# Score and meta products over all 128 array rows, and head pairs side by side, in a four-layer kernel

## The chip, the cores and the metric

The kernel runs on one core of a Trainium2 chip. TensorE multiplies (a weight load puts the stationary operand into its 128 x 128 array, a matmul streams the moving operand through it), VectorE (DVE) and ScalarE (ACT) work on what it leaves in PSUM, GpSimd (POOL) does small jobs in SBUF, SyncE (SP) issues DMAs. The metric is the device time of one execution in microseconds (us), the median of several runs.

## What is computed

Two small transformers run one after the other on 256 tokens of width 1024, in float32. The first has layer A (latent attention with a gated convolution), an MLP, layer C (sparse attention over compressed, selected and windowed keys) and an MLP. The second sees the 256 tokens behind 16 meta tokens and has layer AB (attention over selected keys, beside gated linear attention) and layer CD (retention beside stick-breaking attention). With 256 tokens all four blocks of layer C are always selected and its window reaches every earlier token. Cut to what the change touches:

```python
# layer C, group g, head r of a group
sc = q @ kc.T * scale - slope * (t - centre)     # compressed keys, 15 of them
o_cmp = softmax(sc) @ vc
o_slc = softmax(q @ ks.T * scale - slope * dist) @ vs
o_win = softmax(q @ kw.T * scale - slope * d) @ vw
out = g0 * o_cmp + g1 * o_slc + g2 * o_win
# layer AB: choice of the keys, attention, gated linear attention
score = einsum('qhs,qh->qs', relu(iq @ ik.T), iw)        # 8 heads of 64, top 64 keys are kept
oa = softmax(aq @ ak.T * scale + bias) @ av              # 8 heads of 64, meta keys among them
ob = tril(q_t @ k_t.T) @ v + q_t @ S_before              # 4 heads, chunks of 64
# layer CD
oc = (q @ k.T * decay) @ v                               # 4 heads of 64, values of 128
od = stick_breaking(dq @ dk.T) @ dv                      # 8 heads of 64
```

## The kernel before, in words

Everything is held transposed: features on the 128 partitions, tokens along a row. Weight matrices stream from HBM in halves of 512 KB; ACT and DVE split each into a high and a low part (lines 289 and 290), and the projections (`proj`, `take2`, `tiles2`, `acc_block`) multiply three of the four products of parts (`mm3`). Operands of type float32r go through TensorE once, plain float32 operands show as two matmuls each. Nearly every matmul is issued by the helper `mm` (line 328), so rows are told apart by their tiles. The program is handed to a scheduler that sets the order of each engine's instructions; each engine then works its list in that order. PSUM has eight banks: two called `d`, two called `m`, four called `w`.

A matmul uses as many rows of the array as its operands have partitions, and as many columns as its stationary operand is wide. The profile gives this as rows*columns: 128*128 for a projection, 64*128 for a product over one head of 64, 32*128 or 16*128 for products over meta or compressed keys, 128*64 where one head's values are the stationary operand.

What the change touches, by line:

- **Layer C** (`layer_c`, line 905 on). For a pair p of heads, `nsa_scores` takes for each head and each half t of the queries a product with the high part of the keys (`kh`, 128 rows: the queries' high part sits on 64 of them, their low part on the other 64) and one with the low part (`kl`, the 64 rows of the head alone) into the same PSUM tile, 256 keys wide for t = 0 and 512 for t = 1. `nsa_compress` makes the compressed keys and values once, the values masked by head into `vbd` (four DVE instructions, line 1068). `nsa_out` starts a pair's output with one product of `vbd` and the compressed weights `pct` over 32 rows, then multiplies with values per head (128*64).
- **Layer AB** (`layer_ab`). `select` takes the 8 products of `iq` and `ik` one by one for each half of the queries, each over 64 rows. `dsa_scores` takes a pair's scores per head and half, each into a PSUM bank of its own; pairs 0 to 2 use `w` banks, pair 3 the two `d` banks. `dsa_out` starts with a product of `vb` and `pmt` over 32 rows. `gla` works through a pair of heads one after the other: scores (`kg`, `qg`, 64 rows), a mask on DVE, products with values, products with the states `st` (64*64).
- **Layer CD** (`layer_cd`). `stick_pair` already puts the two heads of a pair side by side. `stick_out` starts with a product of `vb` and `wm` over 32 rows; `retention` starts a head's output with two products of `am` and the meta values over 16 rows.

Of the kernel before, what the change touches and what calls it, by code (L numbers as in the profile page):

```python
# [86 lines left out]
def _const_c():  # L87
# [18 lines left out]
    half = ((np.arange(128)[:, None] // 16) % 2 == np.arange(2)[None, :]).astype(np.float64)  # L106
# [46 lines left out]
def _const_cd():  # L153
# [17 lines left out]
    half = np.zeros((128, 2))  # L171
    for i in range(64):
        rep[15 - i % 16, i] = 1.0
        half[i, (i // 16) % 2] = 1.0
# [135 lines left out]
class K:  # L310
# [593 lines left out]
    def layer_c(self, xh, xl):  # L904
        nc, tc = self.nc, self.tc
        with tc.tile_pool(name="lc", bufs=1) as lp, tc.tile_pool(name="lc2", bufs=2) as l2:
# [5 lines left out]
            cw, cs = tile([128, 96], "cw"), tile([128, 516], "cs")  # L912
# [7 lines left out]
            kbd, vbd = tile([128, 2, 32], "kbd"), tile([128, 2, 2, 64], "vbd")  # L920
# [5 lines left out]
            for gp in range(2):  # L926
# [40 lines left out]
            self.nsa_gates(xh, xl, r, cs[:, 512:514], gt, lp)  # L967
            self.nsa_compress(self.psum("d"), blk, w1, cw, cs[:, 514:516], kbd, vbd, lp)
# [26 lines left out]
    def nsa_gates(self, xh, xl, r, has, gt, lp):  # L995
# [3 lines left out]
        ge = lp.tile([48, SEQ], F32, name="ge")  # L999
# [33 lines left out]
    def nsa_compress(self, ps, blk, w1, cw, half, kbd, vbd, lp):  # L1033
# [25 lines left out]
        for gg, s in enumerate(HALVES):  # L1059
            nc.vector.tensor_copy(kbd[s, :, 16 * gg:16 * gg + 16], kp[s].rearrange("p (gp n) -> p gp n", gp=2))  # L1060
        hr = lp.tile([128, 2, 4, 32], F32, name="hr")
        nc.vector.tensor_copy(
            hr[64:128], hg[64:128].rearrange("p gp gg n -> p gp (gg n)")[:, :, None, :].broadcast_to([64, 2, 4, 32]))
        for gp in range(2):
# [30 lines left out]
    def nsa_scores(self, p, q2, kh, kl, gt, l2, bank):  # L1095
# [6 lines left out]
        for gg in range(2):  # L1102
            st = l2.tile([128, 2, 2, 2], F32, tag=f"st{gg}", name=f"st{gg}")
            h = HALVES[gg]
            pm = []
            for t in range(2):
# [3 lines left out]
                self.mm(s, q[h], kl[h, gp, :256 * (t + 1)], False, True)  # L1110
# [31 lines left out]
    def nsa_out(self, p, pts, vt, vbd, pct, mh, ml):  # L1142
        gp, r = p // 4, p % 4
        o = self.psum("m")[:, :SEQ]
        q = slice(32 * r, 32 * r + 32)
        self.mm(o, vbd[q, gp].rearrange("p g d -> p (g d)"), pct[q, gp].rearrange("p t n -> p (t n)"), True, False)
# [24 lines left out]
    def values(self, xh, xl, r, pool, l2, name):  # L1171

        v = pool.tile([128, 3, 512], F32, tag="tok", name=name)
        tmp = []
# [173 lines left out]
    def select(self, nz, ps, r, mk, iq, gp, l2):  # L1348
# [32 lines left out]
    def gla(self, j, qg, kg, kdt, bvt, dec, cau, mix, gp):  # L1381
# [20 lines left out]
        for hf in range(2):  # L1402
            h = 2 * j + hf
            hs = slice(64 * hf, 64 * hf + 64)
            p = self.psum("w")
            for t in range(2):
                ts = slice(16 + 128 * t, 144 + 128 * t)
                self.mm(p[:, 128 * t:128 * t + 128], kg[hs, j, ts], qg[hs, j, ts])
            self.mm(p[0:16, 256:272], kg[hs, j, 0:16], qg[hs, j, 0:16])
# [5 lines left out]
            o = self.psum("w")[:, :384]  # L1415
            vs = slice(128 * h, 128 * h + 128)
# [3 lines left out]
            for c in range(4):  # L1420
                self.mm(o[64 * (c % 2):64 * (c % 2) + 64, 128 * (c // 2):128 * (c // 2) + 128],
                        qg[hs, j, 16 + 64 * c:80 + 64 * c], st[hs, c], False, c >= 2)
            ob = gp.tile([128, 384], F32, tag="gob", name="gob")
# [21 lines left out]
    def dsa_meta(self, aq, ak, avt, skew, rep, half, dp):  # L1445
# [4 lines left out]
        vb = dp.tile([32, 4, 2, 64], F32, tag="vb", name="vb", bufs=1)  # L1450
        pv = p.rearrange("p (a b c) -> p a b c", a=4, b=2)
        for g in range(2):
            nc.vector.tensor_scalar(vb[:, :, g], pv[:, :, g], half[0:32, g:g + 1], None, op0=OP.mult)
# [24 lines left out]
    def dsa_scores(self, pr, aq, ak, skew, mk, dp, bank):  # L1478
# [3 lines left out]
        pmeta = dp.tile([128, 2, 2, 16], F32, tag="pmeta", name="pmeta")  # L1482
        for g in range(2):
            h = 2 * pr + g
            hs = slice(64 * g, 64 * g + 64)
# [30 lines left out]
        pmt = dp.tile([32, 256], F32, tag="pmt", name="pmt")  # L1516
        nc.scalar.activation(pmt, p[0:32, :256], AF.Copy)
# [25 lines left out]
    def layer_cd(self, xh, xl, x):  # L1543
# [3 lines left out]
        with tc.tile_pool(name="cd", bufs=1) as lp, tc.tile_pool(name="cd2", bufs=2) as l2, \  # L1547
                tc.tile_pool(name="cd4", bufs=4) as l4:
            tile = lambda shape, name: lp.tile(shape, F32, name=name)
            ccd = tile([128, 2 * T2 + 3 * 128 + 66], "ccd")  # L1550
# [6 lines left out]
            cuts = np.cumsum([0, T2, T2, 128, 128, 128, 64, 2]).tolist()  # L1557
# [87 lines left out]
            vb = tile([64, 4, 2, 64], "vb")  # L1645
            for g in range(2):
                nc.vector.tensor_scalar(vb[:, :, g], p.rearrange("p (a b c) -> p a b c", a=4, b=2)[:, :, g],
                                        half[0:64, g:g + 1], None, op0=OP.mult)
# [3 lines left out]
            self.stick_out(0, wts, vb, dvr, mix, l2)  # L1652
            stick(2)
            rotary(cq, r, S)
            cvt = self.values(xh, xl, r, l2, l2, "cvt")
            ret = lambda j: self.retention(j, ck, cq, cvt, dect, l2)
# [235 lines left out]
```

## Time and profile before

| what | us |
|---|---|
| median of 3 runs (1009.80 to 1014.47) | 1012.83 |
| the profiled execution, device time | 1015.24 |
| its span, first to last instruction | 1013.5 |
| PE busy, of the span | 986.9 |
| DVE busy | 669.7 |
| ACT busy | 517.6 |
| POOL busy | 86.2 |

The profile is one execution. Busy time of PE is modelled from sizes, and matmuls overlap in a pipeline, so the duration of a row says little; what a matmul costs is read from the start of one row to the start of the next. A row of the timeline merges neighbours of one kind (x2), and the time to the next row's start is then that of all of them. PEclk is the clock granted to TensorE as a share of its full 2.4 GHz; 0.50 is its other level, 1.2 GHz.

### The profile page before, as it was taken

What the parts mean: (1) busy time and instruction counts of PE and PEld (TensorE: products, weight loads), DVE (VectorE), ACT (ScalarE), POOL (GpSimd) and SP (SyncE); (2) the same over time, 40 slices, a digit from 0 to 9 for tenths busy, and PEclk for the clock granted to TensorE, in tenths of its full rate; (3) what the DMA queues carried; (4) which work ended last, traced back from release to release, by engine and by line L of the source; (5) the groups of instructions that cost most, each with busy time, mean ns of one, the idle gap of its engine ahead of it and who ended that gap; (6) DMA issues with size and microseconds to landing.
All of it is one profiled execution on the core that took longest, in us unless ns stands there. A gap on an engine that the chain in (4) does not pass through costs nothing.

```text
span 1013.5 us, 19176 instructions
## 1 busy us (share of the span) xinstructions
PE 986.9 (97%) x7638; PEld 913.8 (90%) x7638; DVE 669.7 (66%) x1372; ACT 517.6 (51%) x933; POOL 86.2 (9%) x112
## 2 busy tenths in 40 slices
PE   7999999999999989999999999999999999999996
PEld 6999989999998967877999999988898679998985
DVE  6889486555555898674855555568977655757752
ACT  6646365444444667564644444455535335454442
POOL 1120010000001000001000000010211201003121
PEclk9999999999999999899899999999999789999999
DMA  9744347555553544211465555547354213643301
GB/s 331 246 163 146 133 139 266 169 193 200 185 172 116 189 156 139 95 58 42 132 235 197 181 175 181 191 143 240 111 172 137 94 43 98 235 129 122 105 1 42
DMA packets 46074, 154.64 MB, mean 153 GB/s; under 512 B 6424, under 2 KB 7968, under 8 KB 45856
## 3 DMA queue, kind: packets, MB, share of 16 engines
q1 hardware_dynamic: 45552, 152.85, 45.1%
q8 instruction: 60, 0.98, 0.4%
q10 hardware_dynamic: 432, 0.57, 0.2%
q14 instruction: 30, 0.25, 0.1%
HBM read 152.33 MB, written 2.70 MB: 153 GB/s over the span
## 4 chain that ended last, share of the span: by engine, by line
PE 94%; DVE 2%; DMA 1%; ACT 1%; issue 1%; POOL 1%; SPq 0%; POOLq 0%; ACTq 0%; DVEq 0%
PE pd L328 46%; PE pw L328 39%; PE pm L328 6%; PE pm L1133 1%; PE pm L1165 1%; DMA x<-in_xT 1%; DMA st<-in_ab_in 1%; POOL rc L389 0%; DVE st L290 0%; PE pm L1506 0%; DVE x L521 0%; PE pm L1704 0%; DVE zz L1027 0%; ACT st L289 0%; PE pw L881 0%
## 5 line engine op out<-in xcount | busy, mean ns | idle before, releaser
L290 DVE TENSOR_TENSOR st<-st,st 128x1024 fp32r<-128x1024 f32 (+2 forms) x274 | 326.6, 1210 | 168.9 <-ACT st L289 168.4
L289 ACT ACTIVATE st<-st 128x1024 fp32r<-128x1024 f32 (+2 forms) x274 | 279.5, 1041 | 276.4 <-PE pd L328 138.8
L328 PE MATMUL pd<-xh,st 128*128 128x256 f32 (+1 forms) x1856 | 360.0, 288 | 8.6 <-ACT st L289 6.3
L328 PEld LDWEIGHTS pd<-xh,st 128*128 128x128 f32 x1856 | 295.4, 191 | 16.7 <-ACT st L289 6.3
L328 PE MATMUL pd<-xl,st 128*128 128x256 f32 (+1 forms) x928 | 265.6, 288 | 0.0
L328 PE MATMUL pw<-hh,st 128*128 128x256 f32 x1024 | 188.4, 283 | 0.0
L328 PEld LDWEIGHTS pd<-xl,st 128*128 128x128 f32 x928 | 177.3, 191 | 2.5 <-issue 1.0
L328 PEld LDWEIGHTS pw<-hh,st 128*128 128x128 f32 x1024 | 161.1, 191 | 0.0
L328 PE MATMUL pw<-hl,st 128*128 128x256 f32 x512 | 144.6, 283 | 0.0
L328 PEld LDWEIGHTS pw<-hl,st 128*128 128x128 f32 x512 | 98.0, 191 | 0.0
L328 PE MATMUL pd<-akq,st 128*128 128x272 f32 (+1 forms) x384 | 78.0, 293 | 0.0
L328 PE MATMUL pw<-xh,st 128*128 128x256 f32 (+1 forms) x384 | 75.1, 285 | 0.8 <-ACT xh L533 0.8
L328 PEld LDWEIGHTS pd<-akq,st 128*128 128x128 f32 x384 | 61.0, 188 | 2.5 <-issue 1.9
L328 PEld LDWEIGHTS pw<-xh,st 128*128 128x128 f32 x384 | 61.2, 189 | 1.4 <-ACT xh L533 1.2
L328 PE MATMUL pd<-gs,st 128*128 128x272 f32 (+1 forms) x192 | 55.3, 288 | 0.0
L328 PE MATMUL pw<-xl,st 128*128 128x256 f32 (+1 forms) x192 | 53.9, 283 | 0.0
L328 PE MATMUL pw<-mh,st 128*128 128x256 f32 x256 | 51.1, 294 | 0.1
L389 POOL TENSOR_TENSOR rc<-rc,mhalf 128x2 f32<-128x2 f32 (+4 forms) x17 | 21.2, 1254 | 323.1 <-DVE rc L386 319.1
L328 PEld LDWEIGHTS pw<-mh,st 128*128 128x128 f32 x256 | 41.8, 197 | 1.3 <-issue 0.6
L487 POOL TENSOR_TENSOR sq<-sq 128x256 f32<-128x256 f32 x12 | 8.9, 740 | 336.1 <-ACT sq L485 335.2
L328 PE MATMUL pw<-ml,st 128*128 128x256 f32 x128 | 37.2, 297 | 0.0
L328 PEld LDWEIGHTS pd<-gs,st 128*128 128x128 f32 x192 | 36.2, 189 | 0.5 <-issue 0.4
(450 smaller groups left out, 1366.8 us busy)
## 6 DMA issues: line engine op xcount, KB each, us to landing
st<-in_w SPq DMA_DIRECT2D x128, 512.0 KB, 4.5
st<-in_ab_in SPq DMA_DIRECT2D x32, 512.0 KB, 3.9
st<-in_cd_in SPq DMA_DIRECT2D x28, 512.0 KB, 4.5
st<-in_a_in SPq DMA_DIRECT2D x18, 512.0 KB, 6.9
st<-in_c_in SPq DMA_DIRECT2D x16, 512.0 KB, 4.6
st<-in_a_out SPq DMA_DIRECT2D x8, 512.0 KB, 5.2
st<-in_c_out SPq DMA_DIRECT2D x8, 512.0 KB, 3.8
st<-in_ab_out SPq DMA_DIRECT2D x8, 512.0 KB, 3.8
```

The source lines that it names most:

```text
L289: self.last = self.nc.scalar.activation(hi[:, p], raw[:, p], AF.Copy).ins
L290: self.nc.vector.tensor_tensor(lo[:, p], raw[:, p], hi[:, p].bitcast(F32), op=OP.subtract)
L328: self.pe = self.nc.tensor.matmul(out, lhsT, rhs, start=start, stop=stop, skip_group_check=True).ins
L389: nc.gpsimd.tensor_tensor(r, r, self.mhalf[:p, :n], op=OP.pow)
L487: add = lambda e, a, b: e.tensor_tensor(self.sqs[a], self.sqs[a], self.sqs[b], op=OP.add)
L1133: nc.tensor.transpose(tp[:, 128 * j:128 * j + 128], src, self.ident)
L1165: nc.tensor.transpose(ps[:b - a, 128 * j:128 * j + 128], x[:, a:b], self.ident)
```

## The change

1. Products over few rows become products over all 128 rows, with zeros in the rows that do not belong: `kl` gets a copy per head that is zero on the other head's 64 rows; `vbd` becomes a tile of eight masked copies of the values for each two key groups, of which a pair of heads multiplies two with all of `pct`; `vb`, `pmt`, `wmt`, `am` and the meta part of `cvt` are 128 rows high and cleared on POOL. Two DVE instructions on 128x512 replace the four of line 1068.
2. Products over 64 rows are issued in pairs, one head on the upper and one on the lower half of the array, into two PSUM banks: in `select`, in `dsa_scores` (where both halves of the queries now share one bank per head), and in `gla` (scores of both heads, then masks, then values, then states alternating between the heads).
3. Three scratch tiles move into rotating buffers that exist already (`ge`, `hr`, `vbd`).

```diff
             kh = lp.tile([128, 2, 2, 512], F32R, name="kh")
-            kl = lp.tile([128, 2, 512], F32R, name="kl")
+            kl = lp.tile([128, 2, 2, 512], F32R, name="kl")
+            for gg, h in enumerate(HALVES):
+                nc.gpsimd.memset(kl.bitcast(F32)[HALVES[1 - gg], :, gg], 0.0)
...
-                    nc.vector.tensor_tensor(kl[h, gp], k[h], kh[h, gp, gg].bitcast(F32), op=OP.subtract)
+                    nc.vector.tensor_tensor(kl[h, gp, gg], k[h], kh[h, gp, gg].bitcast(F32), op=OP.subtract)
...
-            for gg in range(2):
-                nc.vector.tensor_scalar(vbd[:, gp, gg], vp, half[:, gg:gg + 1], None, op0=OP.mult)
+
+            v = self.pair(SEQ, "sq", bufs=4).rearrange("p a (b d) -> p (a b) d", d=64)
+            nc.vector.tensor_tensor(v, vp[:, None, :].broadcast_to([128, 8, 64]),
+                                    half[:, :, None].broadcast_to([128, 8, 64]), op=OP.mult)
+            vbd.append(v)
...
-                self.mm(s, q[h], kl[h, gp, :256 * (t + 1)], False, True)
+                self.mm(s, q, kl[:, gp, gg, :256 * (t + 1)], False, True)
...
-        self.mm(o, vbd[q, gp].rearrange("p g d -> p (g d)"), pct[q, gp].rearrange("p t n -> p (t n)"), True, False)
+        self.mm(o, vbd[gp][:, 2 * r:2 * r + 2].rearrange("p g d -> p (g d)"), pct[:, gp].rearrange("p t n -> p (t n)"),
+                True, False)
...
-                hs = slice(64 * (h % 2), 64 * (h % 2) + 64)
-                p = self.psum("w")[:, :wd]
-                self.mm(p, iq[hs, h // 2, 16 + 128 * t:144 + 128 * t], ik[hs, :wd])
+
+                if h % 2 == 0:
+                    two = [self.psum("w")[:, :wd] for _ in range(2)]
+                    for p, hs in zip(two, HALVES):
+                        self.mm(p, iq[hs, h // 2, 16 + 128 * t:144 + 128 * t], ik[hs, :wd])
+                p = two[h % 2]
...
+        ps, os2, ats = [[self.psum("w") for _ in range(2)] for _ in range(2)] + [[]]
+        for t in range(2):
+            ts = slice(16 + 128 * t, 144 + 128 * t)
+            for p, hs in zip(ps, HALVES):
+                self.mm(p[:, 128 * t:128 * t + 128], kg[hs, j, ts], qg[hs, j, ts], t == 0, False)
...
-            for c in range(4):
+        for c in range(4):
+            for o, hs in zip(os2, HALVES):
                 self.mm(o[64 * (c % 2):64 * (c % 2) + 64, 128 * (c // 2):128 * (c // 2) + 128],
                         qg[hs, j, 16 + 64 * c:80 + 64 * c], st[hs, c], False, c >= 2)
...
-        vb = dp.tile([32, 4, 2, 64], F32, tag="vb", name="vb", bufs=1)
+        vb = dp.tile([128, 4, 2, 64], F32, tag="vb", name="vb", bufs=1)
+        self.pmts = [dp.tile([128, 256], F32, name=f"pmt{i}", bufs=1) for i in range(2)]
+        for v in (vb, *self.pmts):
+            nc.gpsimd.memset(v, 0.0)
...
+        parts = (0, 0, 144), (1, 144, 416)
+        ss = [self.psum(bank)[:, :416] for _ in range(2)]
+        for t, c, d in parts:
+            for s, hs in zip(ss, HALVES):
+                self.mm(s[:, c:d], aq[hs, pr, 16 + 128 * t:144 + 128 * t], ak[hs, pr, :d - c], t == 0, t == 1)
...
-            for t, wd in ((0, 144), (1, 272)):
-                s = self.psum(bank)[:, :wd]
-                self.mm(s, aq[hs, pr, 16 + 128 * t:144 + 128 * t], ak[hs, pr, :wd])
+            for t, c, d in parts:
+                s, wd = ss[g][:, c:d], d - c
...
+            vb = tile([128, 4, 2, 64], "vb")
+            wmt, am = tile([128, 256], "wmt"), tile([128, 2, 256], "am")
+            for v in (vb, wmt, am):
+                nc.gpsimd.memset(v, 0.0)
...
-            self.mm(o, vb[32 * pr:32 * pr + 32, P].rearrange("p a b -> p (a b)"), wm[32 * pr:32 * pr + 32], True, False)
+            self.mm(o, vb[:, P].rearrange("p a b -> p (a b)"), wm, True, False)
...
-                self.mm(o[:, c:c + 128], am[:, f, 128 * t:128 * t + 128], cvt[0:16, 0, vs], c == 0, False)
+                self.mm(o[:, c:c + 128], am[:, f, 128 * t:128 * t + 128], cvt[:, 0, vs], c == 0, False)
```

## Rows read from the trace of the kernel before

**Rows 1.** The page: span, busy time of PE, the chain that ended last by engine, and the costliest group of weight loads (busy us, mean ns of one, idle before it).

```profile
span 1013.5 us, 19176 instructions
PE 986.9 (97%) x7638; PEld 913.8 (90%) x7638; DVE 669.7 (66%) x1372; ACT 517.6 (51%) x933; POOL 86.2 (9%) x112
...
PE 94%; DVE 2%; DMA 1%; ACT 1%; issue 1%; POOL 1%; SPq 0%; POOLq 0%; ACTq 0%; DVEq 0%
...
L328 PEld LDWEIGHTS pd<-xh,st 128*128 128x128 f32 x1856 | 295.4, 191 | 16.7 <-ACT st L289 6.3
```

**Rows 2.** Busy time of each engine by stretch (us from the span's start, length, then PE, PEld, DVE, ACT, POOL busy, the granted clock, DMA share, GB/s): the two parts of layer C's attention, and two of the stretches with the lower clock, in layer C and in layer AB.

```profile
366.00:424.00 58.00, 58.00 (x348) 44.40 (x346) 48.17 (x170) 38.94 (x108) 0.00 (x0) 0.99 0.42 137
424.00:478.00 54.00, 53.19 (x383) 43.20 (x382) 31.25 (x125) 30.78 (x98) 2.22 (x3) 0.95 0.17 55
422.60:429.40 6.80, 6.80 (x28) 5.85 (x28) 3.09 (x16) 2.94 (x11) 0.00 (x0) 0.50 0.19 59
798.10:818.50 20.40, 20.40 (x90) 12.11 (x87) 8.06 (x31) 3.52 (x13) 2.41 (x4) 0.50 0.08 27
```

**Rows 3.** Timeline of PE in layer C (start us, duration us, engine, line, operation, tiles, rows*columns, shape, count).

```profile
402.76 0.40 PE L328 MATMUL pd<-xh,st 128*128 128x256 f32 x2
403.00 0.28 PE L328 MATMUL pw<-kh,q 128*128 128x256 f32 x1
403.21 0.38 PE L328 MATMUL pw<-kl,q 64*128 64x256 f32 x1
403.52 0.38 PE L328 MATMUL pd<-xl,st 128*128 128x256 f32 x1
403.74 0.40 PE L328 MATMUL pd<-xh,st 128*128 128x256 f32 x2
404.06 0.69 PE L328 MATMUL pm<-pct,vbd 32*128 32x256 f32 x2
404.69 1.52 PE L328 MATMUL pm<-pt,vt 128*64 128x256 f32 x16
...
406.56 0.49 PE L328 MATMUL pw<-kl,q 64*128 64x512 f32 x1
406.99 0.39 PE L328 MATMUL pd<-xl,st 128*128 128x256 f32 x1
```

**Rows 4.** All matmuls of the tiles `kl` and `vbd` (least, median and longest ns, first and last start, shapes).

```profile
L328 PE MATMUL pw<-kl,q x20: 379/436/792, 370.2 to 423.4; 64*128 64x256 f32 x10, 64*128 64x512 f32 x10
...
L328 PE MATMUL pd<-kl,q x12: 380/437/506, 421.5 to 455.0; 64*128 64x256 f32 x6, 64*128 64x512 f32 x6
...
L328 PE MATMUL pm<-pct,vbd x16: 374/426/478, 404.1 to 469.5; 32*128 32x256 f32 x16
```

**Rows 5.** Timeline of PE in layer A: plain float32 products over all 128 rows; the x8 are four matmuls of 128 columns and four of 256 (1,536 columns), the x4 half of that (768).

```profile
80.07 1.47 PE L328 MATMUL pw<-kt,qt 128*128 128x128 f32 x8
81.38 0.38 PE L881 MATMUL pw<-cg,sm 128*128 128x128 f32 x2
...
94.99 0.82 PE L328 MATMUL pd<-kt,qt 128*128 128x128 f32 x4
95.74 0.87 PE L328 MATMUL pm<-pts,vt 128*64 128x256 f32 x8
```

**Rows 6.** By line: DVE on 128x512 out of PSUM (count | busy us, mean ns of one | idle before), and the longest POOL memsets (least, median, longest ns).

```profile
L940 DVE TENSOR_TENSOR qt<-pd,rq 128x512 f32<-128x512 f32 x4 | 2.8, 689 | 0.4 <-PE pd L328 0.3
...
L715 POOL MEMSET qt<- x4: 514/517/519, 0.7 to 2.4; 32x512 f32 x4
```

**Rows 7.** Timeline of PE in `select`: the first and the last of the six stretches in which the eight products of width 272 stand (the eight of width 144 stand in five).

```profile
713.56 0.73 PE L328 MATMUL pw<-ik,akq 64*128 64x272 f32 x4
714.22 0.40 PE L328 MATMUL pd<-xl,st 128*128 128x272 f32 x1
...
725.21 0.72 PE L328 MATMUL pw<-ik,akq 64*128 64x272 f32 x2
725.86 0.39 PE L328 MATMUL pd<-xh,st 128*128 128x272 f32 x1
```

**Rows 8.** Timeline of PE in `dsa_scores`: one head of pair 0 (a product of width 144 and one of 272, two passes each), and both heads of pair 1 in one stretch.

```profile
765.14 0.97 PE L328 MATMUL pw<-akq 64*128 64x144 f32 x4
766.04 0.40 PE L328 MATMUL pd<-xh,st 128*128 128x272 f32 x1
...
769.62 0.98 PE L328 MATMUL pw<-akq 64*128 64x144 f32 x8
770.53 0.39 PE L328 MATMUL pd<-xh,st 128*128 128x272 f32 x1
```

**Rows 9.** Timeline of PE: one product of width 272 of `dsa_scores` for pair 3 inside the stretch with the lower clock, and one head's scores in the second `gla`.

```profile
800.19 1.27 PE L328 MATMUL pd<-akq 64*128 64x272 f32 x2
801.39 0.69 PE L328 MATMUL pw<-bvt,kdt 64*64 64x128 f32 x4
...
830.07 0.85 PE L328 MATMUL pw<-gs,kg 64*128 64x128 f32 x6
830.85 0.39 PE L328 MATMUL pw<-bvt,gat 16*16 16x128 f32 x2
```

**Rows 10.** Timeline of PE in layer CD: the products of one head's `am` with the meta values.

```profile
962.33 0.71 PE L328 MATMUL pw<-cvt,am 16*128 16x128 f32 x4
962.97 0.39 PE L328 MATMUL pd<-akq,st 128*128 128x256 f32 x1
```

More of the change, by code (lines that the diff above doesn't have):

```diff
@@ L105, in _const_c @@
     has = (t >= 31).astype(np.float64).reshape(2, 128).T
-    half = ((np.arange(128)[:, None] // 16) % 2 == np.arange(2)[None, :]).astype(np.float64)
+    half = (np.arange(128)[:, None] // 16 == np.arange(8)[None, :]).astype(np.float64)
     small = np.concatenate([cmpb.reshape(128, 512), has, half], 1)
@@ L170, in _const_cd @@
     rep = np.zeros((128, 64))
-    half = np.zeros((128, 2))
+    half = np.zeros((128, 4))
     for i in range(64):
         rep[15 - i % 16, i] = 1.0
-        half[i, (i // 16) % 2] = 1.0
+        half[i, i // 16] = 1.0
     return (np.concatenate([c_, s, perm, anti, mask, rep, half], 1).astype(np.float32),
@@ L993, in layer_c, with nsa_gates @@
             self.out_proj(mh, ml, acc)
-    def nsa_gates(self, xh, xl, r, has, gt, lp):
+    def nsa_gates(self, xh, xl, r, has, gt, l2):
         nc = self.nc
@@ L1031, in nsa_blocks, with nsa_compress @@
         return blk
-    def nsa_compress(self, ps, blk, w1, cw, half, kbd, vbd, lp):
+    def nsa_compress(self, ps, blk, w1, cw, half, kbd, lp, l2):
         nc = self.nc
@@ L1169, in by_token, with values @@
                 nc.scalar.activation(dst[:b - a, t], ps[:b - a, :128 * n], AF.Copy)
-    def values(self, xh, xl, r, pool, l2, name):
+    def values(self, xh, xl, r, pool, l2, name, zero=False):
         v = pool.tile([128, 3, 512], F32, tag="tok", name=name)
+        if zero:
+            self.nc.gpsimd.memset(v[:, 0], 0.0)
         tmp = []
@@ L1401, in gla @@
         jk = gp.tile([128, 128], F32, tag="gjk", name="gjk")
[L1402 to L1409, printed above, removed]
+        ps, os2, ats = [[self.psum("w") for _ in range(2)] for _ in range(2)] + [[]]
[3 more added lines that the diff above has]
+                self.mm(p[:, 128 * t:128 * t + 128], kg[hs, j, ts], qg[hs, j, ts], t == 0, False)
+        for p, hs in zip(ps, HALVES):
+            self.mm(p[0:16, 256:272], kg[hs, j, 0:16], qg[hs, j, 0:16], False, True)
+        for p in ps:
             at = gp.tile([128, 272], F32, tag="gat", name="gat")
@@ L1414, in gla @@
             nc.vector.tensor_tensor(at[0:16, 256:272], p[0:16, 256:272], cau[0:16, 0:16], op=OP.mult)
-            o = self.psum("w")[:, :384]
-            vs = slice(128 * h, 128 * h + 128)
+            ats.append(at)
+        for hf, (o, at) in enumerate(zip(os2, ats)):
+            vs = slice(128 * (2 * j + hf), 128 * (2 * j + hf) + 128)
             for t in range(2):
@@ L1515, in dsa_scores @@
             nc.tensor.transpose(p[0:32, 128 * t:128 * t + 128], pmeta[:, t].rearrange("p a b -> p (a b)"), self.ident)
-        pmt = dp.tile([32, 256], F32, tag="pmt", name="pmt")
-        nc.scalar.activation(pmt, p[0:32, :256], AF.Copy)
+        pmt = self.pmts[pr % 2]
+        nc.scalar.activation(pmt[0:32], p[0:32, :256], AF.Copy)
         return pts, pmt
@@ L1644, in layer_cd @@
             self.mm(p, rep[0:16], dvt[0:16, 0])
[L1645 to L1648, printed above, removed]
+            vb = tile([128, 4, 2, 64], "vb")
+            wmt, am = tile([128, 256], "wmt"), tile([128, 2, 256], "am")
+            for v in (vb, wmt, am):
+                nc.gpsimd.memset(v, 0.0)
+            nc.vector.tensor_tensor(vb[0:64].rearrange("p (q a) b c -> p q (a b) c", q=2),
+                                    p.rearrange("p (q m c) -> p q m c", q=2, c=64),
+                                    half[0:64, None, :, None].broadcast_to([64, 2, 4, 64]), op=OP.mult)
             stick(1)
@@ L1651, in layer_cd @@
             rotary(ck, rk, slice(0, T2))
-            self.stick_out(0, wts, vb, dvr, mix, l2)
+            self.stick_out(0, wts, vb, dvr, mix, wmt)
             stick(2)
             rotary(cq, r, S)
-            cvt = self.values(xh, xl, r, l2, l2, "cvt")
-            ret = lambda j: self.retention(j, ck, cq, cvt, dect, l2)
+            cvt = self.values(xh, xl, r, l2, l2, "cvt", True)
+            ret = lambda j: self.retention(j, ck, cq, cvt, dect, am, l2)
             stick(3)
@@ L1660, in layer_cd @@
             silu(mix[:, 0:2])
-            self.stick_out(1, wts, vb, dvr, mix, l2)
+            self.stick_out(1, wts, vb, dvr, mix, wmt)
             ret(1)
@@ L1710, in stick_pair, with stick_out @@
             wts[h] = w
[L1712 removed]
+    def stick_out(self, q, wts, vb, dvr, mix, wm):
         nc = self.nc
@@ L1717, in stick_out @@
                                 self.ident)
-        wm = l2.tile([64, 256], F32, tag="wmt", name="wmt")
-        nc.vector.tensor_copy(wm, p[:, :256])
+        nc.vector.tensor_copy(wm[0:64], p[:, :256])
         for pr in range(2):
```

30 lines of the change are left out of this document (14 added, 16 removed).

## The prediction

> **What bounds the kernel now.** I read the page first: PE is busy for 97% of the span and makes 94% of the chain that ended last [rows 1]. A busy PE need not be a well used one, so next I read its timeline by the starts of the rows, and the table of stretches for who else is near his limit. In layer C's attention PE has no gap from 366 to 424 us and under 1 us from 424 to 478, while DVE is busy for 48.17 of 58 us in the first part and 31.25 of 54 in the second [rows 2]. So PE's time is the kernel's time there, with DVE 9.8 us behind it in the first part. The same table shows the clock granted at 0.50, the lower level of 1.2 GHz, in 422.6 to 429.4 and 798.1 to 818.5 us [rows 2]. Before the first fall PE alternated between `kh` and `kl` [rows 4]; during the second it ran products over parts of the rows [rows 9].
>
> **Layer C, the low parts.** In a stream of 128*128 products of width 256 a matmul follows the other after 0.12 us (two in 0.24 from 402.76) [rows 3]. Around a `kl` the starts are 0.21 (`kh`, then the switch to 64 rows), 0.31 (`kl`) and 0.22 (the first after it), together 0.74 instead of 0.36: 0.38 us lost for one product over half the rows [rows 3]. A `kl` of width 512 takes 0.43 where twice 0.12 would do, which is again 0.19 over [rows 3]; I give it the same entry and exit, so 0.38 as well. There are 16 such products of each width, no second pass, 32 in all [rows 4]. With zeros in the other 64 rows they become products like `kh`, the stream never leaves 128*128, and the sum is 32 x 0.38 = 12.2 us of PE. The bounds for one are 0 (the cost comes with the extra operand, not with the rows) and 0.38; I take the upper, since the neighbours `kh` stand in the same stream, with the same weights and widths.
>
> Here one rule speaks against the change. The row is that a 128x128 load takes 191 ns [rows 1] and yet the products start every 0.12 us [rows 3], so it is hidden behind the matmul before. The Trainium skill, "TensorE: Matmul & The Clock Gate", Part 3 (The mechanism), says that a weight load overlaps running matmuls only when its row group differs; by that every load over 128 rows would stand open, and `kl` would gain nothing. The starts 0.12 apart contradict it for full rows.
>
> **Layer C, the compressed values.** `vbd` over 32 rows takes 0.63 us for its two passes (404.06 to 404.69) and its entry shows in the two matmuls before it, 0.32 instead of 0.24 [rows 3]: 0.71. Plain float32 over all rows costs 1.31 us for 1,536 columns, 0.85 ns a column [rows 5], so 2 x 256 columns are 0.44; going from there to the 128*64 products costs 0.75 - 768 x 0.85 ns = 0.10 [rows 5]. That is 0.54, a gain of 0.17 on each of the 8 (16 matmuls, [rows 4]): 1.4 us.
>
> **Layer C, the rest.** Two DVE instructions on 128x512 at 0.69 us [rows 6] replace four on a quarter of the columns each, at most 1.4 us more, early in the first part; `vbd` is needed only at 404 [rows 3], so it costs nothing unless DVE is full. The two POOL memsets on `kl` are 1,024 elements a row, two times 0.517 us each [rows 6], on a POOL that has nothing to do in 366 to 424 [rows 2]; they stand before the first scores and I give them nothing (0 to 1 us, if the wait for their space held up the normalisation's POOL step). `ge`, `hr` and `vbd` in rotating buffers can add a wait of DVE for PE's last read; bounds 0 and 1 us, taken 0, since those reads are early.
>
> What of the 12.2 + 1.4 us reaches the end? 22 of the 32 `kl` lie before 424, 8.4 us; PE would then need about 49.6 us beside DVE's 48.2 plus up to 1.4. Two engines that feed one another do not run both full, so I take 5 of 8.4 (bounds 2 and 8.4). After 424 DVE has 22 us to spare [rows 2]: 10 x 0.38 + 1.4, taken 5. The stretch 422.6 to 429.4 at half clock holds 3.4 us of full-clock work [rows 2]; before it fell, 64-row products stood among the rest, and they are gone. I take 3 (bounds 0 and 3.4). **Layer C: 13 us**, bounds 7 and 17.
>
> **Layer AB at the full clock.** What a pair costs is in the trace: one head's two products take 0.90 us, both heads' take 0.91 when they stand together [rows 8]; the second half of the array is free. Leaving and entering 128*128 costs 0.09 + 0.10 each time, from the `kl` rows. In `select` the products of width 272 stand in six stretches, alone 0.65, paired 0.66 [rows 7], those of width 144 in five; four of each are left. That is 2 x (0.65 + 0.19) + 1 x (about 0.45 + 0.19) = 2.3 us. In `dsa_scores` pairs 1 and 2 can't gain, the rows are already side by side; pair 0 gains 0.90 + 0.19 = 1.1, pair 3, in four stretches, 0.90 + 3 x 0.19 = 1.5. In `gla` a head's scores take 0.78 [rows 9]; two of four vanish, 1.6, with four switches, 0.8; the products with the states are over 64*64 already and I give their new order nothing (0 to 1.5). The four `pmt` give 0.17 each, 0.7. Sum 8.0 us. The PSUM banks of `gla` are a wait that the change adds: the outputs need the two banks of the states' products, behind them in PE's list are the values; they are read by DVE before the masks anyway, so 0, at most 0.5 each.
>
> **Layer AB's lower clock.** Of these 8 us, pair 3, one `gla`'s scores and one `pmt` lie in the 20.4 us at 0.50: 1.5 + 1.2 + 0.2 = 2.9, which there are worth 5.8; a product of width 272 takes 1.20 instead of 0.65 [rows 7, 9]. DVE (8.06 of 20.4) and ACT (3.52) are idle most of it [rows 2], so PE sets the pace. If the clock stays down over the same work, layer AB gains 8.0 + 2.9 = 10.9. If it stays up, the stretch's work shrinks by 20.4 / 2 = 10.2 as well, and layer AB gains 18.2. I take the second: before the fall PE had left the projections for products over 16, 32 and 64 rows, and exactly these are now done in pairs, over all rows, or in half as many stretches. Bounds for the clock's part: 2.9 and 10.2.
>
> **Layer CD.** The products of `am` take 0.64 for four passes, plus 0.19 for the switches, against 4 x 128 x 0.85 ns = 0.44 [rows 5, 10]: 0.39 x 4 = 1.6. `wmt` gives up to 0.17 x 4 = 0.7. Memsets on POOL of 512 and 256 elements are 0.5 and 0.3 us by the same row [rows 6]. Taken 1.8 of 2.3.
>
> **Sum.** 13 + 18.2 + 1.8 = 33 us. The profiled execution took 1015.24 us (span 1013.5), so it would take 982. The median of the runs is 1012.83, 2.4 us lower; 33 off it gives 980. I say 981.
>
> **Rivals.**
> 1. *The clock in layer AB stays down.* The attention's chain still has no projections in it, and PE may wait between its steps. For it: the stretch lies at the end of the layer's projections. Price 18.2 - 10.9 = 7.3: 25.7 gained, 988.
> 2. *DVE becomes the bound in layer C.* It is 83% busy in the first part [rows 2] and gets more. Then the first part gives 2, the waiting PE keeps its lower clock near 424 (0), and layer C gives 7; if layer AB keeps half its 8 and its clock too, the gain is 7 + 6 + 1.5 = 14.5: 999.
> 3. *Full rows don't do what the change says.* If each `kl` over 128 rows waits openly for its weights (0.19 load, 0.12 product), it costs its 0.31 as before, and only pairs, `pmt` and half a clock stretch gain: 8 + 2 = 10, 1004. Against it: `kh` [rows 3]. It is what the rule on weight loads in the Trainium skill, "TensorE: Matmul & The Clock Gate", Part 3, would give.
> 4. *Slower.* PE, waiting for DVE, loses the full clock over long stretches. Each us of full-clock work then costs one more. Without any gain from the clock the change saves 10 + 8 + 1.8 = 20; the kernel is slower from 20 us of full-clock work, 40 us of lowered clock, more than now, most of the first part of layer C. At 50 us it is 1018. Against it: the clock held through 366 to 422 with the same DVE.
>
> **How the numbers follow.** Forecast 0.50, rival 1 0.27, rival 2 0.13, rival 3 0.06, rival 4 0.04. The forecast's own range is 974 to 987 (layer C 9 to 17, AB 15 to 19); rival 1 adds up to 993, rival 2 up to 1000. 974 to 1000 leaves out rivals 3 and 4 and tails, about 0.17. A measurement of this kernel tells about 0.5%, 5 us, from no change. Faster by more than that: all but rival 4 and a tail of 2 and 3, 0.92; within: 0.05; slower 0.03.
>
> **What would show it.** After the change no `kl` row has 64*128, and starts around it are 0.12 and 0.24; `vbd` takes 0.44; all `select` products stand in fours; the `dsa_scores` of pairs 0 and 3 take about 0.91; no stretch at 0.50 near 422 or 798. DVE's idle time in layer C's first part falls below 5 us. I am wrong if 128-row products with zeros start 0.3 apart, or if the scheduler's new order puts PE's waits where it had projections.

## The result, and the profile after

The changed kernel took 983.37 us, the median of four runs (982.60 to 986.22), beside 1011.32 us for the kernel before on the same chip: a ratio of 0.9734 with a 95% interval of 0.9686 to 0.9782. The forecast was 981. Five more runs in a second comparison gave 984.48 beside 1004.30, 0.9797 (0.9772 to 0.9822). The ratios leave out executions more than 1.5% above the fastest of their kernel.

The profiled execution took 982.69 us, against 1015.24. The page of the changed kernel, from its first lines, and the chain that ended last by engine:

```profile
span 980.9 us, 19189 instructions
...
PE 956.9 (98%) x7638; PEld 898.9 (92%) x7638; DVE 667.9 (68%) x1369; ACT 515.9 (53%) x933; POOL 92.0 (9%) x121
...
PE 93%; DVE 3%; ACT 1%; DMA 1%; issue 1%; POOL 1%; SPq 0%; POOLq 0%; DVEq 0%; ACTq 0%
```

PE still is the kernel's time, with the same 7,638 matmuls; it has 30.0 us less to do by the page [rows 1]. By stages, busy time in the changed kernel (columns as in [rows 2]): the first part of layer C as before, layer C from its first `kh` product to the sums of squares behind it, layer AB from sums to sums, layer CD, and the longest stretch at 0.50 (1.2 GHz) within the span, at the hand-over from the MLP to layer AB.

```profile
366.00:424.00 58.00, 57.55 (x416) 49.87 (x416) 54.01 (x214) 46.80 (x141) 0.00 (x0) 1.00 0.41 132
...
364.90:458.70 93.80, 92.10 (x696) 78.94 (x694) 75.01 (x286) 67.85 (x204) 3.24 (x6) 1.00 0.33 109
670.20:841.80 171.60, 171.60 (x1336) 152.61 (x1335) 130.84 (x341) 82.02 (x166) 25.32 (x43) 1.00 0.43 144
...
841.80:972.91 131.11, 131.11 (x984) 117.72 (x983) 82.00 (x160) 58.38 (x118) 28.01 (x23) 1.00 0.29 93
...
651.80:658.60 6.80, 6.56 (x20) 4.34 (x21) 4.46 (x13) 2.04 (x4) 0.48 (x1) 0.50 0.53 160
```

The same three stages in the kernel before, cut at the same instructions:

```profile
369.98:477.74 107.76, 106.95 (x696) 83.54 (x694) 75.90 (x286) 68.40 (x204) 2.22 (x3) 0.97 0.28 92
688.86:872.25 183.39, 182.77 (x1334) 159.14 (x1333) 131.06 (x342) 82.63 (x166) 24.63 (x40) 0.94 0.41 136
872.25:1005.49 133.24, 133.24 (x987) 118.59 (x985) 81.43 (x161) 58.75 (x118) 24.60 (x22) 1.00 0.28 92
```

Layer C's attention lost 13.96 us, layer AB 11.79, layer CD 2.13. Note the column of the granted clock: 0.97 and 0.94 before, 1.00 after. Part of these differences is the clock of two single executions, and the experiments had to separate it from the work. The profiled execution of the kernel before, 1015.24 us, is slower than each of the 61 executions of it that were timed beside the experiments (996.98 to 1014.48).

Layer C in the changed kernel, PE's timeline (as [rows 3]) and the tile `kl` (as [rows 4]):

```profile
403.75 0.36 PE L328 MATMUL pw<-kh,q 128*128 128x256 f32 x1
403.96 0.28 PE L328 MATMUL pw<-kl,q 128*128 128x256 f32 x1
404.07 0.28 PE L328 MATMUL pd<-kh,q 128*128 128x256 f32 x1
404.19 0.28 PE L328 MATMUL pd<-kl,q 128*128 128x256 f32 x1
404.31 0.97 PE L328 MATMUL pw<-kbd,qt 128*128 128x32 f32 x8
405.12 0.48 PE L328 MATMUL pd<-kh,q 128*128 128x512 f32 x1
405.43 0.39 PE L328 MATMUL pd<-kl,q 128*128 128x512 f32 x1
405.67 0.81 PE L1140 MATMUL pm<-cg,pm 128*128 128x128 f32 x6
...
416.63 0.59 PE L328 MATMUL pm<-pct,sq 128*128 128x256 f32 x2
417.16 0.44 PE L328 MATMUL pm<-pt,vt 128*64 128x256 f32 x2
```
```profile
L328 PEld LDWEIGHTS pw<-kl,q x20: 186/189/193, 364.9 to 410.6; 128*128 128x128 f32 x20
L328 PE MATMUL pw<-kl,q x20: 278/338/398, 365.0 to 410.8; 128*128 128x256 f32 x10, 128*128 128x512 f32 x10
```

From start to start a `kl` of 256 takes 0.11 to 0.12 us and one of 512 0.24, where they took 0.31 and 0.43 [rows 3]. Its weight load of 189 ns is hidden behind the matmul before. This is where the time went, as the rows of the weight loads show, first in the kernel before, then in the changed one:

```profile
406.56 0.18 PEld L328 LDWEIGHTS pw<-kl,q 64*128 64x128 f32 x1 [0.24 <-issue]
406.99 0.19 PEld L328 LDWEIGHTS pd<-xl,st 128*128 128x128 f32 x1 [0.24 <-issue]
```
```profile
404.08 0.19 PEld L328 LDWEIGHTS pd<-kl,q 128*128 128x128 f32 x1
```

Before, the load of a `kl` starts together with its product (406.56, [rows 3]), after 0.24 us without any load, and the same holds for the full-row product behind it (406.99). After, the load of the `kl` of 404.19 starts at 404.08, while the matmul before it runs. In the kernel before the load starts 1 to 2 ns ahead of the product for all 32 `kl`, and 1 to 3 ns ahead for all 32 products behind them; in the changed kernel the load of a `kl` starts 110 to 236 ns ahead in 31 of 32. `vbd` (the tile `sq`) takes 0.53 to the next start, with the change to 128*64 in it.

Layer AB in the changed kernel: products of `select`, of `dsa_scores` (pairs 1 and 3), and a `gla`'s scores.

```profile
694.25 0.73 PE L328 MATMUL pw<-ik,akq 64*128 64x272 f32 x4
696.49 0.72 PE L328 MATMUL pw<-ik,akq 64*128 64x272 f32 x2
...
749.21 0.97 PE L328 MATMUL pw<-akq 64*128 64x144 f32 x6
757.64 0.72 PE L328 MATMUL pw<-akq 64*128 64x272 f32 x2
...
778.70 0.71 PE L328 MATMUL pw<-gs,kg 64*128 64x128 f32 x8
...
780.18 0.52 PE L328 MATMUL pd<-akq 64*128 64x144 f32 x4
780.63 0.44 PE L328 MATMUL pw<-bvt,kdt 64*64 64x128 f32 x4
780.99 0.73 PE L328 MATMUL pd<-akq 64*128 64x272 f32 x4
```

An x2 is one head alone (two passes), an x4 a pair. `gla`'s scores do stand together (x8). But `select` still has lone products: its stretches hold as many rows as before, 4, 2, 2, 2, 4, 2 of width 272. Pair 1 of `dsa_scores`, side by side before [rows 8], is now torn: six rows at 749.21, the other head's 272 eight us later. The order of the program didn't decide which products became neighbours; the scheduler did. That it goes by the PSUM bank that comes free is my reading, and no run tests it.

### The profile page after: what moved, and what is told of

Its sections match the earlier page's. It is cut to its first block, busy times and chain, and to the rows that moved or that the text cites. A ratio compares the mean times of both kernels' runs of the same rounds, so it can differ in the third digit from the quotient of the medians.

```text
span 980.9 us, 19189 instructions
## 1 busy us (share of the span) xinstructions
PE 956.9 (98%) x7638; PEld 898.9 (92%) x7638; DVE 667.9 (68%) x1369; ACT 515.9 (53%) x933; POOL 92.0 (9%) x121
## 4 chain that ended last, share of the span: by engine, by line
PE 93%; DVE 3%; ACT 1%; DMA 1%; issue 1%; POOL 1%; SPq 0%; POOLq 0%; DVEq 0%; ACTq 0%
PE pd L328 45%; PE pw L328 38%; PE pm L328 6%; DVE st L290 1%; PE pm L1140 1%; PE pm L1172 1%; DMA st<-in_c_v 1%; DMA x<-in_xT 1%; ACT pm L1126 0%; POOL rc L389 0%; DVE zz L1030 0%; PE pm L1528 0%; PE pm L1730 0%; DVE x L521 0%; PE pw L881 0%
## 5 line engine op out<-in xcount | busy, mean ns | idle before, releaser
L328 PE MATMUL pw<-mh,st 128*128 128x256 f32 x256 | 48.7, 285 | 0.3 <-ACT mh L340 0.2
L328 PEld LDWEIGHTS pw<-xl,st 128*128 128x128 f32 x192 | 36.3, 189 | 0.0
```

The source lines that it names most:

```text
L328: self.pe = self.nc.tensor.matmul(out, lhsT, rhs, start=start, stop=stop, skip_group_check=True).ins
```

## The experiments

To separate work from clock I use the span times the mean granted clock of an execution, called **work** here. It means something because PE bounds nearly all of the span. For the kernel before it is 990.6 us over the 61 timed executions beside the experiments, with a standard deviation of 1.3, while their times differ by 17.5 us. The rest of the span is what the lower clock took. A mean over four to six executions is thus good to some 0.6 us, and a difference in work below about 1 us says nothing. The table holds all timed executions.

| kernel | executions | median us | mean clock (range) | work us |
|---|---|---|---|---|
| before | 61 | 1004.70 | 0.987 (0.975 to 0.996) | 990.6 |
| changed | 4 + 5 | 983.37, 984.48 | 0.993 (0.992 to 0.996) | 975.7 |
| c_scores_alone, _again | 4 + 12 | 991.05, 995.28 | 0.988 (0.978 to 0.996) | 980.3 |
| layer_c_alone | 6 | 993.11 | 0.989 (0.978 to 0.996) | 979.7 |
| ab_pairs_alone | 10 | 1002.92 | 0.989 (0.980 to 0.996) | 990.2 |
| gla_alone | 10 | 999.73 | 0.991 (0.985 to 0.996) | 987.9 |
| zero_rows_alone | 4 | 996.56 | 0.989 (0.986 to 0.993) | 984.2 |
| all_but_c_scores | 9 | 997.67 | 0.989 (0.986 to 0.992) | 984.9 |
| old_gla | 5 | 986.22 | 0.993 (0.989 to 0.996) | 977.1 |
| old_dsa_scores | 6 | 983.38 | 0.992 (0.989 to 0.995) | 974.2 |
| select_zero_rows | 6 | 980.63 | 0.993 (0.991 to 0.996) | 971.5 |
| select_dsa_zero_rows | 6 | 983.56 | 0.993 (0.991 to 0.995) | 974.8 |

**c_scores_alone, c_scores_again.** The kernel before with

```diff
-                self.mm(s, q[h], kl[h, gp, :256 * (t + 1)], False, True)
+                self.mm(s, q, kl[:, gp, gg, :256 * (t + 1)], False, True)
```

and `kl` as in the change.

> The kernel before, with only the products of kl over 128 rows (and ge and hr in rotating buffers, to make room). Theory 1 (each lone product over 64 rows costs 0.38 us for leaving and entering 128*128, and the half-clock stretch near 423 us goes with them): 32 x 0.38 = 12.2, plus 3.4 for the clock, layer C 14 to 16 us shorter, no other layer changes. Rival (much of layer C's 17 us came from a new order of the scheduler, from vbd or from the waits ahead of zz): 4 to 9 us.

> The kernel before with kl over 128 rows once more, for its mean clock. Work at the full clock as before, 980 to 981.5 us. If the scores of layer C are what lets the clock fall, the mean clock comes near that of the changed kernel, 0.993; if several stages do, it lies between the two, 0.989 to 0.991.

Measured: ratios 0.985 (0.9778 to 0.9923) and 0.9904 (0.9869 to 0.9939). The work fell by 10.3 us, nearly two below the 12.2 of the first theory; the clock, 0.988, is nearly that of the kernel before. So the first theory has the clock wrong. By time the first comparison gave 14.8 us and would have confirmed it; the second gave 8.6. Neither case for the clock came in c_scores_again, whose own mean was 0.987.

**all_but_c_scores.** The changed kernel with the line above turned back.

> The changed kernel, with kl back on 64 rows. Theory 1: 14 to 16 us slower than the changed kernel, 12 to 14 us faster than the kernel before; the half-clock stretch in layer C's attention is back. Rival (order of the scheduler): 4 to 9 us slower than the changed kernel.

Measured: a ratio of 0.9905 (0.9867 to 0.9942), 984.9 us of work, 9.2 over the changed kernel. By time it is 13 to 14 us slower than the changed kernel, near what the first theory said, but over 4 of these are clock; and it is 8 us faster than the kernel before, not 12 to 14. Its profile has no lowered stretch inside layer C's attention, where the theory wanted one. Its layer AB holds the changed kernel's matmuls in the same order and takes 172.55; the 0.95 us over 171.60 are one longer step 9 us behind the sums. So single profiles of one program can differ by 1 us in a stage.

**ab_pairs_alone, zero_rows_alone.** By an error in their making both held the wrong `gla`: the first has the new `select` and `dsa_scores` but the old `gla`, the second has the products over all rows (not `kl`) and the new `gla`. They are read as that.

```diff
-                p = self.psum("w")[:, :wd]
-                self.mm(p, iq[hs, h // 2, 16 + 128 * t:144 + 128 * t], ik[hs, :wd])
+                    for p, hs in zip(two, HALVES):
+                        self.mm(p, iq[hs, h // 2, 16 + 128 * t:144 + 128 * t], ik[hs, :wd])
```

> The kernel before, with only the pairs of layer AB (select, dsa_scores, gla); pmt, vb and all of layers C and CD as before. Theory 1 (pairs shorten layer AB by themselves and keep the clock up near 798 us): 10 to 11 us faster, no long stretch at 0.50 in layer AB. Rival (it is the products over 16 and 32 rows that let the clock fall): the stretch at 0.50 stays, and 1 to 4 us are gained.

> The kernel before, with only the products of meta and compressed values over all rows (vbd, pmt with vb, wmt, am), none of the pairs and kl on 64 rows. Theory 1: 8 x 0.17 + 0.7 + 2.1 = 4 us faster, both half-clock stretches stay (423 and 798 us). Rival (these products over few rows are what lets the clock fall in layer AB): 14 us faster, the stretch near 798 us gone.

Measured: 0.9959 (0.9926 to 0.9992) and 0.9892 (0.9838 to 0.9947), the work 0.4 and 6.4 us under the kernel before. Neither number answers its theories, since `gla` was in the other kernel. The profile of the first is worth more than its time: its layer C is that of the kernel before, instruction for instruction, and it ran at the full clock. Layer C's attention and layer AB in ab_pairs_alone:

```profile
366.46:471.16 104.70, 103.88 (x695) 80.86 (x694) 76.46 (x288) 68.40 (x204) 2.22 (x3) 1.00 0.29 99
680.52:854.44 173.92, 173.92 (x1336) 154.30 (x1335) 130.93 (x342) 82.07 (x166) 23.73 (x40) 1.00 0.43 143
```

and in c_scores_alone, whose layer AB is that of the kernel before:

```profile
368.17:462.90 94.73, 93.38 (x696) 79.23 (x694) 73.39 (x286) 67.40 (x204) 2.22 (x3) 1.00 0.31 104
673.33:847.30 173.97, 173.91 (x1334) 154.36 (x1332) 130.62 (x342) 82.56 (x166) 24.72 (x40) 1.00 0.42 143
```

The unchanged program thus takes 104.70 in layer C and 173.97 in layer AB when the clock holds; 107.76 and 183.39 were those stages with the clock down. So the stretches of 6.8 and 20.4 us [rows 2] don't come with every execution, though the first came in more than one: gla_alone, with the same layer C, has it again at 420.3 to 427.1. The change's work is 104.70 to 93.80 and 173.97 to 171.60. The pairs of `select` and `dsa_scores` by themselves give 0.05.

**gla_alone, old_gla.** The new `gla` in the kernel before, and the old one in the changed kernel:

```diff
-                self.mm(p[:, 128 * t:128 * t + 128], kg[hs, j, ts], qg[hs, j, ts])
+            for p, hs in zip(ps, HALVES):
+                self.mm(p[:, 128 * t:128 * t + 128], kg[hs, j, ts], qg[hs, j, ts], t == 0, False)
```

> The kernel before with the new order of gla alone. Theory 1: 2.4 us less work at the full clock than the kernel before, 988.5, and by its clock's part a mean clock above that of the kernel before. Rival (the order of the scheduler around it gives more): 3 to 4 us less, 987 to 988. If lowered clock comes by execution, the mean clock is that of the kernel before within 0.003.

> The changed kernel with gla as in the kernel before. Theory 1 (two of four stretches of scores vanish, 1.6, with four switches, 0.8): 2.4 us more work at the full clock than the changed kernel, 978 to 979. Rival (the order of the scheduler gives or takes more than the pairs): 3.5 us or more over it, or none.

Measured: 0.9941 (0.9913 to 0.9969) and 0.9815 (0.9789 to 0.984); the work 2.7 less, and 1.4 more. Layer AB in gla_alone, and in zero_rows_alone, which has `pmt` over all rows as well:

```profile
685.74:856.67 170.93, 170.93 (x1334) 152.43 (x1332) 129.94 (x342) 82.28 (x166) 24.70 (x40) 1.00 0.42 145
```
```profile
682.32:852.95 170.63, 170.60 (x1334) 152.34 (x1332) 129.97 (x342) 82.26 (x166) 25.90 (x43) 1.00 0.43 146
```

`gla` gives 3.0 of layer AB's 173.97 in the kernel before, and its work of 987.9 is what its rival said (987 to 988); `pmt` gives 0.3. In the changed kernel `gla` gives less: the 1.4 lie between the theory (2.4) and its rival (none, or 3.5), with an error of about 1. The mean clock of gla_alone, 0.991, is 0.003 over that of the kernel before in the same comparison (0.988), at the edge of what the last sentence allowed.

**old_dsa_scores, changed_again.** The changed kernel with the old `dsa_scores`, and the changed kernel itself once more.

```diff
-        ss = [self.psum(bank)[:, :416] for _ in range(2)]
+                s = self.psum(bank)[:, :wd]
```

> The changed kernel with dsa_scores as in the kernel before (one head at a time, a bank for each half). Theory 2 (what the pairs of dsa_scores save, 0.7 us, is less than the 2.3 us by which the way from the first of these scores to the first gla scores got longer): 1 to 2 us less work at the full clock than the changed kernel, 974 to 975. Theory 1 (pairs 0 and 3 save 1.1 + 1.5): 2 to 3 us more, 978 to 979.

> The changed kernel once more, for more executions beside the kernel before on one chip. The measure is the span times the mean granted clock (work at the full clock) and the mean clock itself. The runs so far give 990.9 us at a mean clock of 0.986 for the kernel before (19 executions) and 976.0 at 0.994 for the changed one (4). Theory 2 (a lowered clock belongs to an execution, not to a stage of the program; the change is worth 15 us and the rest of the difference is which executions were profiled and compared): mean clock again 0.986 to 0.989, median 986 to 990 us. Rival (the change keeps the clock up in nearly every execution): mean clock 0.993 or more, median 982 to 985.

Measured: 0.979 (0.9762 to 0.9819) and 0.9797 (0.9772 to 0.9822). Layer AB in old_dsa_scores, and in changed_again:

```profile
672.35:842.92 170.57, 170.57 (x1334) 152.38 (x1333) 129.84 (x341) 82.27 (x166) 25.86 (x43) 1.00 0.42 144
```
```profile
673.15:844.76 171.61, 171.61 (x1335) 152.61 (x1334) 130.83 (x342) 82.01 (x166) 25.29 (x43) 1.00 0.42 145
```

The pairs of `dsa_scores` cost 1.0 us here (171.60 to 170.57, and 974.2 of work, as theory 2 said), and with the old `gla` they gave 0.05 together with `select`; forecast were 2.6. The times to the next start, added up by tile, show where: the products of `dsa_scores` themselves take 0.7 less in the changed kernel (4.90 beside 5.61), but the products with `bvt` beside them 0.75 more and the projections 0.56 more. On the clock my second theory fell: the changed kernel kept 0.992 to 0.995 in five further executions.

**layer_c_alone.** `kl` and `vbd` as in the change, layers AB and CD as before.

```diff
-        self.mm(o, vbd[q, gp].rearrange("p g d -> p (g d)"), pct[q, gp].rearrange("p t n -> p (t n)"), True, False)
+        self.mm(o, vbd[gp][:, 2 * r:2 * r + 2].rearrange("p g d -> p (g d)"), pct[:, gp].rearrange("p t n -> p (t n)"),
+                True, False)
```

> All of the change in layer C (kl and vbd over all rows, the scratch tiles moved), layers AB and CD as before. Work at the full clock: kl 10.5 and vbd 0.8 less than the kernel before, 979 to 980 us. The open question is the clock: c_scores_again had 0.987, as the kernel before, the changed kernel 0.993. If it is the last product over few rows in layer C's attention (vbd) that lets the clock fall there, no profile and few executions lose it in layer C, and the mean clock is about 0.990, with layer AB's part still lost. If it is one thing all over the kernel (no stage by itself), it stays at 0.987.

Measured: 0.9884 (0.9835 to 0.9934), 10.9 us less work (979.7, as expected), clock 0.978 to 0.996. Its profiled attention in layer C:

```profile
366.76:460.65 93.89, 92.20 (x695) 79.04 (x694) 75.00 (x286) 67.87 (x204) 2.21 (x3) 1.00 0.33 109
```

0.8 us less than c_scores_alone: `vbd`. Its mean clock, 0.989, came as the first case said, but with six executions from 0.978 on that doesn't separate the two cases.

**select_zero_rows, select_dsa_zero_rows.** Zeros where pairs had failed, on old_dsa_scores:

```diff
+        ik = gp.tile([128, 2, T2], F32, name="ik")
...
-                self.mm(p, iq[hs, h // 2, 16 + 128 * t:144 + 128 * t], ik[hs, :wd])
+                self.mm(p, iq[:, h // 2, 16 + 128 * t:144 + 128 * t], ik[:, h % 2, :wd])
```

> The changed kernel with dsa_scores as in the kernel before and with the products of select taken one head at a time over all 128 rows (ik in two copies, each with zeros in the other half). By 0.85 ns a column and pass a product of width 272 costs 0.46 us and one of 144 0.245 us; in the changed kernel they stand alone or in fours and sixes at 0.65, 0.66, 0.44 and 0.68, each stretch with 0.09 for its entry. Theory (the order of the scheduler undoes pairs, zeros don't depend on it): 4 x 0.28 - 2 x 0.17 + 3 x 0.28 + 0.1 = 1.7 us less work at the full clock than old_dsa_scores, 972.5. Rival (the switches cost nothing beside the projections): 5.7 in place of 6.4, 0.7 us less.

> As select_zero_rows, and the products of dsa_scores one head at a time over all 128 rows too (ak in two copies with zeros, four more DVE instructions of 64 rows). A head costs 416 x 2 x 0.85 ns = 0.71, eight 5.7, beside 5.6 and some seven entries at 0.09 now. Theory: a further 0.6 us less, 971.9. Rival (the scheduler's order around the scores decides, as it did for the pairs): 2 us more or less than select_zero_rows.

Measured: 0.9754 (0.9708 to 0.98) and 0.9787 (0.9736 to 0.9839). Layer AB in select_zero_rows, and two of the stretches of `select` in it with the product behind each:

```profile
671.36:839.32 167.96, 167.95 (x1333) 153.40 (x1332) 129.39 (x342) 82.17 (x166) 25.94 (x43) 1.00 0.44 148
```
```profile
694.05 1.08 PE L328 MATMUL pw<-ik,akq 128*128 128x272 f32 x4
694.76 0.49 PE L328 MATMUL pd<-xl,st 128*128 128x272 f32 x1
...
696.21 0.29 PE L328 MATMUL pd<-xh,st 128*128 128x272 f32 x1
696.34 0.62 PE L328 MATMUL pw<-ik,akq 128*128 128x272 f32 x2
696.60 0.49 PE L328 MATMUL pd<-xh,st 128*128 128x272 f32 x1
696.92 0.29 PE L328 MATMUL pd<-xl,st 128*128 128x272 f32 x1
```

and the lone product of the changed kernel, with its neighbours:

```profile
696.27 0.29 PE L328 MATMUL pd<-xh,st 128*128 128x272 f32 x1
696.49 0.72 PE L328 MATMUL pw<-ik,akq 64*128 64x272 f32 x2
697.14 0.39 PE L328 MATMUL pd<-xh,st 128*128 128x272 f32 x1
697.37 0.29 PE L328 MATMUL pd<-xl,st 128*128 128x272 f32 x1
```

A lone product takes 0.26 instead of 0.65 to the next start, but the product behind it 0.32 where a stream has 0.13; from the product in front of it to the second behind it is 0.71 instead of 1.10, so 0.39 are saved. A pair's two take 0.71 instead of 0.66. Layer AB is 2.6 us shorter than in old_dsa_scores, more than the 1.7 expected. With zeros in `dsa_scores` too, 2.9 us are lost again (170.84 from sums to sums), as the rival said (2 us or more). By tile the products of `dsa_scores` gain 0.4 there; 1.15 of the loss is one wait of PE for POOL's `kd` (line 1256 of that kernel), and most of the rest is spread over projections and `gla`, with no cause shown. select_zero_rows has the least work of all kernels tried, 4.2 us under the changed one.

## Why the prediction was right, and where its steps were not

The time was right (981, measured 983.4) and so was the sum on the profiled executions (33, measured 32.6), but both with luck. Of the 32.6 us only 27.9 lie in the three stages that the forecast adds up (13.96, 11.79, 2.13); 5.1 lie ahead of layer C's attention, and the change doesn't explain them. And on averages the change is worth 21.6 us, from a kernel before of 1004.7 us: the start of the sum was 8 us too high, the gain 11 too large, and the two nearly cancel. What held best is the price of products over part of the rows in layers C and CD.

**Layer C, work.** Taken 5 + 5 = 10 us at the full clock, of 13.6 that the prices gave; 10.8 came (104.70 to 93.89) in two profiles at 1.00. The others agree: with half of each lowered stretch taken off, the five with `kl` on 64 rows take 104.1 to 104.7, the two with only `kl` changed 94.7 and 94.9, the seven with `vbd` too 93.5 to 93.9. Two errors cancel. A `kl` gives (104.70 - 94.73) / 32 = 0.31 us, not 0.38, and DVE didn't hold PE up: in the first part it is busy 54.01 of 58 us, idle below 5 as foretold, but PE waits for 0.45 only; over the whole attention it waits 1.70 of 93.80, where it was 0.82 of 104.70. `vbd` gave 0.8 of 1.4. A price read at one place [rows 3] was the upper bound of the average.

**Layer C, clock.** Taken 3; in these two executions 107.76 - 104.70 = 3.1. From the layer's first sums of squares to its first `kh` another 3.2 us went (319.34 to 369.98 us before, 317.51 to 364.90 after). ab_pairs_alone, with the old code there, took 47.75 us for it, so 2.9 of these too belong to the execution. 1.8 us more lie ahead of the kernel's first sums (17.0 us from the start before, 15.2 after), which the change doesn't touch.

**Layer AB, work.** This is the step that failed: 8.0 forecast, 173.97 - 171.60 = 2.4 measured. "All `select` products stand in fours" didn't happen (2.3 forecast, 0 measured), and in `dsa_scores` pair 0 and pair 3 came together while pairs 1 and 2, which I had written off as unable to change, were torn: the products gained 0.7 and the work around them lost 1.7 (2.6 forecast, -1.0 measured). `gla` gave 3.0 of 2.4 in the old surroundings, 1.7 of it in its scores and 0.5 in the products with the states, whose new order I had given nothing; in the changed kernel it gave 1.4. `pmt` gave 0.3 of 0.7. I had taken the order of the program for the order on PE. The front of this document says that a scheduler sets it.

**Layer AB, clock.** Taken 10.2; 183.39 - 173.97 = 9.4 in the two profiles. The forecast's reason for it isn't shown: the old code, matmul for matmul, took 173.97 at 1.00 in c_scores_alone. And as a forecast for the median it was too much. The profiled execution lost 20 us to the clock (1013.5 x 0.020), the kernel before loses 13.2 on average, the changed one 6.5. On averages the change is worth 990.6 - 975.7 = 14.9 us of work and 6.7 of clock, not 20 and 13. The median of the first comparison, 1011.32, stood high as well.

**Why the clock is kept** is shown only as frequencies. In layer C's attention the lowered stretch occurs in 3 of 5 profiles with `kl` on 64 rows and 1 of 9 with 128; in layer AB in 3 of 6 with the old `gla` and none of 8 with the new. These are few, and right behind layer C's attention, within 5 us of its end, a lowered stretch stands in 3 of the 5 and in 5 of the 9 as well. The means say more: `kl` alone has 0.988 over 16 executions, everything but `kl` 0.989 over 9, both together 0.993. `gla` alone has 0.991; old_gla, which has everything but `gla`, has 0.993, with one lowered stretch in layer AB. So no part tried brings it by itself, and what the clock reacts to stays open. The lowered stretch near `gla`'s scores in old_gla, and two in c_scores_again, one in each layer:

```profile
803.70:807.10 3.40, 3.40 (x15) 2.82 (x14) 1.33 (x5) 0.78 (x2) 0.00 (x0) 0.50 0.03 7
```
```profile
792.70:796.10 3.40, 3.40 (x23) 2.53 (x20) 1.78 (x6) 1.07 (x6) 0.00 (x0) 0.50 0.00 0
379.70:383.10 3.40, 3.40 (x9) 2.63 (x9) 2.97 (x17) 2.52 (x9) 0.00 (x0) 0.50 0.16 20
```

**Layer CD.** 1.8 forecast, 2.1 measured. A head's products of `am` now take 0.36 to the next start, and the product behind them 0.20 where a stream has 0.12, together the 0.44 of the forecast:

```profile
931.36 0.60 PE L328 MATMUL pw<-cvt,am 128*128 128x128 f32 x4
931.72 0.36 PE L328 MATMUL pd<-akq,st 128*128 128x256 f32 x1
931.92 0.28 PE L328 MATMUL pd<-gs,st 128*128 128x256 f32 x1
```

**The rivals.** In the profiled execution rival 1 (the clock in layer AB stays down) and rival 2 (DVE binds in layer C) didn't occur; the 6 us that rival 2 gives layer AB is not worked out there (half of its 8 is 4). Rival 3 is refuted by the starts at 404.07 and 404.19: a load of 189 ns over full rows is hidden. The open load that it feared for full rows is what the 64 rows of the old `kl` paid. The rule that gave it (the Trainium skill, "TensorE: Matmul & The Clock Gate", Part 3), read as one on all loads, doesn't hold for this stream; the same section also has a load into the background weight buffer pulled ahead of running matmuls, and that agrees with the loads that start 0.11 us ahead. Rival 4 didn't occur: no lowered stretch in layer C's attention in the profile after.

## What to carry to other kernels

In a stream of full-array matmuls a lone product over half the rows costs more than one over all rows with zeros: 0.31 us for `kl`, 0.39 for a lone float32 product of `select`. Zeros shortened the lone products in every place tried, whatever stood beside them, while a pair side by side saves only if nothing comes between. But neither is the whole bill: in `dsa_scores` both shortened the products and lengthened the layer, by what came to stand or wait around them. Before counting on pairs, look in the trace at which instructions became neighbours. And read a lowered clock in one profile as a draw: compare spans times granted clock, and spans, over many executions.

## What the hardware showed that was not expected

A product over half the rows, between products over all rows, has its weight load in the open, and so has the full product behind it; over all rows the same load is hidden. The mean granted clock of the unchanged kernel ran from 0.975 to 0.996 on the same input, 4 to 25 us of a span, and 15 us less work were followed by nearly half as much again in clock, for a reason that stays open. The Trainium skill, "TensorE: Matmul & The Clock Gate", Why this matters for your kernels, says that a single product over 32 rows takes the time of one over 128. That doesn't hold for one between full ones: `vbd` went from 0.71 us with its entry [rows 3] to 0.53, `kl` from 0.31 to 0.12 with less around it. The Trainium skill, "TensorEngine Tiling (Array Packing)", Key Properties, says that a change of tiling mode drains the engine. The rows agree as far as they go: at both changes no load runs ahead of its product, and 0.31 us for going out and back is the price they give on average; the draining itself is in no row.
